# Scan parameters behind u's low parts and squares behind the casts, with TensorE's middle order held by a list

## The chip, the cores and the metric

The kernel runs on one core of a Trainium2 chip. The metric is the device time of one execution in microseconds (us), as the median of several runs; lower is better. The short names of the engines are those of the profile: PE is TensorE's matrix multiplication and PEld its weight load, DVE is VectorE, ACT is ScalarE, POOL is GpSimd, and SP issues most of the DMAs.

## The reference: what is computed

One hybrid decoder block on x with 256 rows of 1024 numbers, all in float32. Two branches run side by side on the same normed projection, are gated and added, and an MLP follows. Cut to what matters here:

```python
h = rms_norm(x, norm_mix_g);  proj = h @ w_in
q, k, v, u, g = split(proj)                       # u: 512 wide
o_a = attention(rotary(q), rotary(k), v)          # 8 heads of 128, causal
step = exp(log_step);  mag = exp(lam_re * step)   # the "scan parameters"
ar, ai = mag * cos(lam_im * step), mag * sin(lam_im * step)
s[t] = a * s[t-1] + c * (b @ u[t])                # 32 groups of 64 complex states
o_b = glu(gelu(real(c_out @ s) + d_skip * u))
x = x + (sigmoid(g_a) * o_a + sigmoid(g_b) * o_b) @ w_out
x = x + square(relu(rms_norm(x) @ w_up)) @ w_down
return rms_norm(x)
```

## The kernel before, in words

Every large product is made of three TensorE products. A weight block is loaded as float32 (tile `raw`), ScalarE rounds it to a high part (`hi`, line 83) and VectorE takes the rest as a low part (`lo`, line 84); the same is done to x (`xgh` on line 172, `xgl` on line 173). TensorE then adds hi by xgh, hi by xgl and lo by xgh. So each weight block costs a DMA, a ScalarE cast, a VectorE subtraction and then its matmuls, and four `hi`, four `lo` and five `raw` buffers turn over.

**Start (lines 117 to 194).** x, g and the weights of u come in first, in eight blocks k = 0 to 7 of 128 rows. The first block's weights come in two halves of 256 columns, the others in 512. `par` holds the scan's parameters (30 KB) and is issued on SP behind block 1's weights. For each block: xgh, xgl, the split of the weights, and 12 matmuls of 256 columns on u_acc (line 186) in the order hi by xgh, hi by xgl, lo by xgh. The squares of x for the norm (`sq`, lines 190 to 194) are ScalarE work, added up on VectorE; line 211 sums them on TensorE (`ms`), and lines 197 to 219 make the inverse root, mostly on POOL. Lines 221 and 222 (`rs_ps`) spread it over the partitions, line 225 copies it to `rs`, and line 239 multiplies u_acc with it to get u. Eight DMAs on ScalarE's queue (line 246) put u into the layout U2.

**Middle (lines 617 to 651).** The order of emission is the list ORDER: V is a half of v's projection (four weight blocks v0 to v3, then v4 to v7, 12 matmuls of 512 columns each), P and C are `prepare()`, the scan's parameters and matrices, T a table of sines, K the projections of q and k for two heads, S, A and G attention and gate, Q the scan of a quarter of the states, B the second gate. `prepare()` starts with some 70 VectorE operations on 128 by 16 numbers (helpers `ts` on lines 388 and 390, `tt` on line 395, `stt` on line 400), each of which mostly needs the one before it; then come multiplications of 128 by 256 (lines 456 to 461), copies to Bs (line 469), transposes `bt` on TensorE (line 486) and their copies W2 (line 487), which the scan's matmuls `x` (line 554) need together with U2.

**End.** glu, the output projection, the MLP's up and down projections, all three-part products as above.

The order on each engine is not written by hand: a scheduler puts the instructions in order with a model of their times and with priorities (a split has `high_priority(SPLIT_PRIO)`, so it goes ahead of other ready work), and the engines then run their lists strictly in that order. `behind(ins, others)` adds an order alone (no semaphore) and `after(...)` an order with a wait.

Of the kernel before, what the change touches and what calls it, by code (L numbers as in the profile page):

```python
# [8 lines left out]
F32 = mybir.dt.float32  # L9
# [34 lines left out]
QK = 2  # L44
ORDER = ("V0 V1 P0 T0 C0 Q0 T1 Q1 T2 K0 T3 X0 S0 G0 A0 G1 K1 K2 S1 Q2 A1 K3 G2 S2 A2 Q3 "
         "B0 G3 S3 X1 Y0 A3 B1")


def build(ctx, tc, dr, out):
    nc = tc.nc  # L50
    V, S, G, PE = nc.vector, nc.scalar, nc.gpsimd, nc.tensor

    keep = ctx.enter_context(tc.tile_pool(name="keep", bufs=1))
    ps = ctx.enter_context(tc.tile_pool(name="ps", bufs=1, space=PSUM))
# [26 lines left out]

    def split(hi, lo, x):
        ins = S.copy(hi, x).ins  # L83
        V.tensor_sub(lo, x, hi.bitcast(F32))  # L84
        return ins

    def mm3(o, wh, wl, xh, xl, first, last, **kw):
        PE.matmul(o, wh, xh, start=first, stop=False, **kw)  # L88
# [74 lines left out]
    V.memset(quarter, 0.25)  # L163
    sq = p1.tile([P, KD, T], F32, tag="yhl", name="sq")
    u_acc = ps.tile([P, 2, 2, T], F32, tag="x", name="u_acc")
    for c in range(4):
        wh = keep.tile([P, 1024], F32R, tag="hi", bufs=HI, name=f"hi_u{c}")
        wl = keep.tile([P, 1024], F32R, tag="lo", bufs=LO, name=f"lo_u{c}")
        for k2 in range(2):
            k, cols = 2 * c + k2, slice(k2 * 512, (k2 + 1) * 512)  # L170
            xk = xT[:, k, :] if k else x0
            S.activation(xgh[:, k, :], xk, AF.Copy, scale=g_mix[:, k : k + 1])
            V.scalar_tensor_tensor(xgl[:, k, :], xk, g_mix[:, k : k + 1],
                                   xgh[:, k, :].bitcast(F32), op0=ALU.mult, op1=ALU.subtract)
            if k:
                last = split(wh[:, cols], wl[:, cols], u_raw[c][:, cols])
                if k == 1:
                    second = last
            else:
                for i in range(2):  # L180
                    part = slice(i * 256, (i + 1) * 256)
                    split(wh[:, part], wl[:, part], u_raw[c][:, part])
            ws = [slice(k2 * 512 + m * P, k2 * 512 + (m + 1) * P) for m in range(4)]
            for i, (w, x) in enumerate(((wh, xgh), (wh, xgl), (wl, xgh))):
                for m in range(4):
                    PE.matmul(u_acc[:, m // 2, m % 2, :], w[:, ws[m]], x[:, k, :],  # L186
                              start=(k == 0 and i == 0 and m % 2 == 0),
                              stop=(k == KD - 1 and i == 2), skip_group_check=True)

    for i, xk in enumerate((x0, xT[:, 1, :])):  # L190
        S.activation(sq[:, i, :], xk, AF.Square)
    for c in range(1, 4):
        S.activation(sq[:, 2 * c : 2 * c + 2, :], xT[:, 2 * c : 2 * c + 2, :], AF.Square)
        V.tensor_add(sq[:, 0:2, :], sq[:, 0:2, :], sq[:, 2 * c : 2 * c + 2, :])


# [21 lines left out]
        rsqrt(G, rs_tok, rsm[:, 0:2], rsm[:, 4:6])  # L218
    V.tensor_scalar(rs_half, rs_tok, 0.5, None, op0=ALU.mult)
    rs_ps = att_bank("rs_ps")  # L220
    for h in range(2):
        PE.matmul(rs_ps[:, 0, h * P : (h + 1) * P], rs_tok[:, h : h + 1].to_broadcast([P, P]),
                  ident, start=True, stop=True)
# [27 lines left out]

    def proj_pair(first, name):
        acc = mm_bank(name)
        for j in range(2):
            wh, wl = in_unit(first + j, name)
            for k in range(KD):
                mm3(acc[:, j, :], wh[:, k * P : (k + 1) * P], wl[:, k * P : (k + 1) * P],
                    xgh[:, k, :], xgl[:, k, :], k == 0, k == KD - 1)
        return acc
# [18 lines left out]

    def tok_proj(first, name):
        other = first == 4  # L280
        acc = [flat(bank("y", 1, f"{name}{first}{h}") if other and h else
                    mm_bank(f"{name}{first}{h}")) for h in range(2)]
        for kk_ in range(4):
            wh, wl = in_unit(first + kk_, name)
            for k2 in range(2):
                k, w = 2 * kk_ + k2, slice(k2 * 512, (k2 + 1) * 512)
                for hf in range(2):
                    tok_mm(acc[hf], wh[:, w], wl[:, w], xgh, xgl, k, hf, k == 0, k == KD - 1)
        return acc
# [20 lines left out]

    def attn_head(q, k, j):
        s = att_bank("s").rearrange("p a b -> p (a b)")
        PE.matmul(s[:, 0:128], q[:, j, 0:128], k[:, j, 0:128], start=True, stop=False,
                  skip_group_check=True)
        PE.matmul(s[:, 0:128], ident_b, tri_b, start=False, stop=True, skip_group_check=True)
        PE.matmul(s[:, 128:384], q[:, j, 128:256], k[:, j, :], start=True, stop=False,
                  skip_group_check=True)
        PE.matmul(s[:, 256:384], ident_b, tri_b, start=False, stop=True, skip_group_check=True)
        st = p1.tile([P, 6], F32, tag="st", bufs=2, name="st")
        V.tensor_reduce(st[:, 0:1], s[:, 0:128], axis=mybir.AxisListType.X, op=ALU.max,  # L320
                        negate=True)
        V.tensor_reduce(st[:, 1:2], s[:, 128:384], axis=mybir.AxisListType.X, op=ALU.max,
                        negate=True)
        pr = p1.tile([P, 384], F32, tag="pr", bufs=2, name="pr")
        act(pr[:, 0:128], s[:, 0:128], AF.Exp, bias=st[:, 0:1],
                     accum_out=st[:, 2:3])
        act(pr[:, 128:384], s[:, 128:384], AF.Exp, bias=st[:, 1:2],
                     accum_out=st[:, 3:4])
        V.reciprocal(st[:, 4:6], st[:, 2:4])
        S.activation(pr[:, 0:128], pr[:, 0:128], AF.Copy, scale=st[:, 4:5])  # L330
        scaled.append(S.activation(pr[:, 128:384], pr[:, 128:384], AF.Copy, scale=st[:, 5:6]).ins)
        return pr

    def attn_pt(pr, last):
        pt = att_bank("pt").rearrange("p a b -> p (a b)")
        for i in range(3):
            after(PE.transpose(pt[:, i * P : (i + 1) * P], pr[:, i * P : (i + 1) * P], ident).ins,
                   last, "a head's transposes together")
        pts = p1.tile([P, 384], F32, tag="pts", bufs=2, name="pts")
        copied.append(S.copy(pts, pt[:, 0:384]).ins)  # L340
        return pts
# [3 lines left out]
    def attn_out(hp, prs, tha):  # L345
        pts = [attn_pt(x, [scaled[2 * hp + j]][: hp < 0]) for j, x in enumerate(prs)]
        o = att_bank("o")
        for j in range(2):
            hd = 2 * hp + j
            after(PE.matmul(o[:, j, :], v[:, 0, hd * P : (hd + 1) * P], pts[j][:, 0:256],  # L350
                             start=True, stop=False, skip_group_check=True).ins,
                   copied[-1:][: hp < 0], "a pair's outputs together")
            PE.matmul(o[:, j, 128:256], v[:, 1, hd * P : (hd + 1) * P], pts[j][:, 256:384],
                      start=False, stop=True, skip_group_check=True)
        V.scalar_tensor_tensor(mixA[:, 2 * hp : 2 * hp + 2, :], tha, 1.0, o,
                               op0=ALU.add, op1=ALU.mult)
# [13 lines left out]
    def prepare():  # L370
# [14 lines left out]
        def ts(x, s1, op0, s2=None, op1=None, o=None):  # L385
            o = t16() if o is None else o
            if op1 is None:
                V.tensor_scalar(o, x, s1, None, op0=op0)
            else:
                V.tensor_scalar(o, x, s1, s2, op0=op0, op1=op1)  # L390
            return o

        def tt(a, b, op):
            o = t16()
            V.tensor_tensor(o, a, b, op=op)
            return o

        def stt(a, s, b, op0, op1):
# [77 lines left out]
        for c in range(2):  # L476
            G.memset(Bs[c], 0.0)
            G.tensor_scalar(Bs[c][:, :, 0:32], bpad[:, c], 1.0, None, op0=ALU.mult)
            place(Bs[c], 32, ab[c], urgent=True)
        W2 = [keep.tile([P, 8, P], F32, tag=f"b4{c}", name=f"W2{c}") for c in range(2)]  # L480
        for c in range(2):
            bsp = Bs[c].rearrange("p (a b) k -> p a (b k)", b=2)
# [22 lines left out]
        Dt = p1.tile([P, 8, P], F32, tag="craw", name="Dt")  # L505
        G.memset(Dt, 0.0)
        dps = att_bank("dps").rearrange("p a b -> p (a b)").rearrange("p (m b) -> p m b", m=4)
        for m in range(4):
            for c, w_ in enumerate((Wr, nWi)):
                PE.matmul(dps[:, m, :], bpad[:, c, 4 * m : 4 * m + 4, :].rearrange("p a b -> p (a b)"),  # L510
# [34 lines left out]
    def ssm_quad(m):  # L545
        W2, mag2 = ssm[0], ssm[-3]
        cs, sn = tabs.pop(m)
        x = ps.tile([P, 2, 2, 2, P], F32, tag="x", name="x")
        xr, xi = [x[:, :, i].rearrange("p j h t -> p h j t") for i in range(2)]
        for h in range(2):  # L550
            for i in range(2):
# [26 lines left out]
        done = V.tensor_add(si, si, w).ins  # L578
        Wr, nWi, Dt = ssm[1:4]
        y = bank("y", 1, "y")  # L580
        for h in range(2):
            p = 2 * m + h
            after(PE.matmul(y[:, h, 0:P], Dt[:, p, :], U2[:, p, 1 : P + 1], start=(h == 0),
# [67 lines left out]
            tok_gate(32 + 4 * n, [thb[2 * n + i] for i in range(2)])  # L651


    mxh = keep.tile([P, KD, T], F32R, tag="b40", name="mxh")
    mxl = keep.tile([P, KD, T], F32R, tag="b41", name="mxl")

# [248 lines left out]
```

## Time and profile before

| | us |
|---|---|
| median of 3 runs (392.59 to 394.09) | 392.66 |
| the profiled execution's own time | 394.03 |
| its span, first to last instruction | 392.2 |
| PE busy | 382.8 (98%) |
| DVE busy | 288.7 (74%) |
| ACT busy | 231.8 (59%) |
| POOL busy | 29.6 (8%) |

The profiled execution has 1.8 us around its span and lies 1.37 us above the median, beside the slowest of the three runs. An instruction's row gives its start in us from the span's start and its length; in square brackets stands how long the engine had been idle before it and what ended that. A busy PE is modelled: the ends of its matmuls overlap the next ones, so the pace is read from one start to the next.

### The profile page before, as it was taken

The page shows a single profiled execution, that of the slowest core. Times are in us where ns is not written, and L with a number is a line of the kernel's source. Part 1 is how long each engine was busy: PE and PEld are TensorE (multiplying, and loading weights), DVE is VectorE, ACT ScalarE, POOL GpSimd, SP SyncE. Part 2 cuts the span into 40 slices and gives each one's busy share as a digit, 9 for nine tenths or more (in the row PEclk, how much of TensorE's full clock was granted, in tenths as well). Part 3 has the DMA queues.
Part 4 walks back from the last instruction along what each step waited for, and adds up shares of the span by engine and source line. Part 5 has one row for each costly group of instructions (what it writes and reads, how often), then busy time and mean ns, then how long its engine had stood idle before and what let it go on. Part 6 is the DMA issues. An engine that isn't in the chain of part 4 may idle for free.

```text
span 392.2 us, 6719 instructions
## 1 busy us (share of the span) xinstructions
PE 382.8 (98%) x2563; PEld 343.7 (88%) x2563; DVE 288.7 (74%) x501; ACT 231.8 (59%) x380; POOL 29.6 (8%) x35
## 2 busy tenths in 40 slices
PE   6999999999999999999999999999999999999993
PEld 3988999999999897888888999999999888888883
DVE  3999979999999997568839676767667444564434
ACT  6769899574554666954646665565555433444313
POOL 4242491000000000000000000000000000000000
PEclk9899999999999999999999999999999999999999
DMA  7993963445435155446486485655655555565202
GB/s 255 355 345 114 263 221 108 162 161 170 165 113 172 62 158 172 161 152 224 161 301 189 140 264 188 203 185 194 210 178 202 188 191 198 185 205 190 82 2 107
DMA packets 23199, 71.57 MB, mean 182 GB/s; under 512 B 2944, under 2 KB 5248, under 8 KB 23168
## 3 DMA queue, kind: packets, MB, share of 16 engines
q1 hardware_dynamic: 20144, 68.92, 51.5%
q10 hardware_dynamic: 3024, 2.23, 1.9%
q8 instruction: 20, 0.33, 0.3%
q14 instruction: 11, 0.09, 0.1%
HBM read 69.18 MB, written 1.05 MB: 179 GB/s over the span
## 4 chain that ended last, share of the span: by engine, by line
PE 92%; DMA 3%; DVE 3%; issue 1%; ACT 0%; SPq 0%; DVEq 0%
PE up L89 7%; PE up L88 7%; PE up L90 7%; PE dn L757 6%; PE dn L756 6%; PE dn L755 6%; PE u_acc L186 3%; DMA x2t<-x 2%; PE gb L272 2%; PE g L88 2%; PE k L88 2%; PE q L88 2%; PE g L89 2%; PE q L89 2%; PE v L272 2%; PE g L90 2%
## 5 line engine op out<-in xcount | busy, mean ns | idle before, releaser
L89 PE MATMUL up<-x2l,hi_up 128*128 128x256 f32 x256 | 70.7, 277 | 0.2 <-DVE x2l L718 0.2
L90 PE MATMUL up<-x2h,lo_up 128*128 128x256 f32 x256 | 70.5, 276 | 0.0
L88 PE MATMUL up<-x2h,hi_up 128*128 128x256 f32 x256 | 70.0, 276 | 0.0
L84 DVE TENSOR_TENSOR lo_dn<-raw_dn,hi_dn 128x1024 fp32r<-128x1024 f32 x32 | 39.2, 1225 | 40.4 <-ACT hi_dn L83 40.4
L83 ACT CAST hi_dn<-raw_dn 128x1024 fp32r<-128x1024 f32 x32 | 33.6, 1050 | 49.1 <-PE dn L757 24.6
L84 DVE TENSOR_TENSOR lo_up<-raw_up,hi_up 128x1024 fp32r<-128x1024 f32 x32 | 38.8, 1224 | 23.4 <-ACT hi_up L83 23.4
L83 ACT CAST hi_up<-raw_up 128x1024 fp32r<-128x1024 f32 x32 | 33.3, 1050 | 34.9 <-PE up L89 16.3
L89 PEld LDWEIGHTS up<-x2l,hi_up 128*128 128x128 f32 x256 | 48.1, 188 | 0.4 <-DVE x2l L718 0.4
L90 PEld LDWEIGHTS up<-x2h,lo_up 128*128 128x128 f32 x256 | 48.1, 188 | 0.0
L88 PEld LDWEIGHTS up<-x2h,hi_up 128*128 128x128 f32 x256 | 47.8, 188 | 0.1
L756 PE MATMUL dn<-lo_dn,hh 128*128 128x512 f32 x96 | 37.4, 389 | 0.0
L757 PE MATMUL dn<-hi_dn,hl 128*128 128x512 f32 x96 | 37.4, 389 | 0.0
L755 PE MATMUL dn<-hi_dn,hh 128*128 128x512 f32 x96 | 37.4, 389 | 0.0
L755 PEld LDWEIGHTS dn<-hi_dn,hh 128*128 128x128 f32 x96 | 18.0, 188 | 3.7
L756 PEld LDWEIGHTS dn<-lo_dn,hh 128*128 128x128 f32 x96 | 18.0, 188 | 3.7
L757 PEld LDWEIGHTS dn<-hi_dn,hl 128*128 128x128 f32 x96 | 18.0, 188 | 3.6
L88 PE MATMUL k<-xgh,hi_k 128*128 128x256 f32 x64 | 18.1, 283 | 0.0
L89 PE MATMUL k<-xgl,hi_k 128*128 128x256 f32 x64 | 18.1, 283 | 0.0
L88 PE MATMUL g<-xgh,hi_g 128*128 128x256 f32 x64 | 18.0, 281 | 0.0
L88 PE MATMUL q<-xgh,hi_q 128*128 128x256 f32 x64 | 17.9, 280 | 0.0
L90 PE MATMUL g<-xgh,lo_g 128*128 128x256 f32 x64 | 17.9, 280 | 0.0
L90 PE MATMUL k<-xgh,lo_k 128*128 128x256 f32 x64 | 17.9, 279 | 0.0
(274 smaller groups left out, 1018.9 us busy)
## 6 DMA issues: line engine op xcount, KB each, us to landing
raw_up<-w_up SPq DMA_DIRECT2D x32, 512.0 KB, 4.3
raw_dn<-w_down SPq DMA_DIRECT2D x32, 512.0 KB, 4.3
raw_v<-w_in SPq DMA_DIRECT2D x8, 512.0 KB, 5.5
raw_q<-w_in SPq DMA_DIRECT2D x8, 512.0 KB, 3.5
raw_k<-w_in SPq DMA_DIRECT2D x8, 512.0 KB, 3.3
raw_g<-w_in SPq DMA_DIRECT2D x8, 512.0 KB, 4.8
raw_gb<-w_in SPq DMA_DIRECT2D x8, 512.0 KB, 3.2
raw_glu<-w_glu SPq DMA_DIRECT2D x8, 512.0 KB, 3.5
```

The costliest lines, as they stand in the source:

```text
L83: ins = S.copy(hi, x).ins
L84: V.tensor_sub(lo, x, hi.bitcast(F32))
L88: PE.matmul(o, wh, xh, start=first, stop=False, **kw)
L89: PE.matmul(o, wh, xl, start=False, stop=False, **kw)
L90: PE.matmul(o, wl, xh, start=False, stop=last, **kw)
L186: PE.matmul(u_acc[:, m // 2, m % 2, :], w[:, ws[m]], x[:, k, :], start=(k == 0 and i == 0 and m % 2 == 0), stop=(k == KD - 1 and i == 2), ...
L272: PE.matmul(acc, xh[:, k, rows], wh, start=first, stop=False)
L755: PE.matmul(acc, xh, wh[:, w], start=(k == lead), stop=False, skip_group_check=True)
L756: PE.matmul(acc, xh, wl[:, w], start=False, stop=False, skip_group_check=True)
L757: PE.matmul(acc, xl, wh[:, w], start=False, stop=(k == end), skip_group_check=True)
```

## The change

Three things. (1) All `ts` and `tt` operations of `prepare()` are put in order behind the VectorE subtraction that makes the low part of u's second block (`second`, k = 1). `stt` and the others follow since they need results of these. (2) The squares of x on ScalarE are put behind casts of u's weights: those of blocks 0 and 1 behind block 0's last cast, those of a pair of later blocks behind the cast of the pair's second block. (3) TensorE's matmuls and transposes from v's first one to the end of the second gate's first part are recorded by name as they are emitted and chained, each behind the one before, in an order that a list of 934 instructions in runs gives. All the orders added are between instructions of one engine, with no semaphore.

```diff
+PE_ORDER = ("v*42 rs*2 v*44 bt*8 q*2 v*10 q*46 bt*8 x*2 k*48 g*13 dps*8 x*6 g*62 x*3 s*8 x*5 "
...
+class Listed:
+    def __init__(self, eng):
+        self.eng, self.name, self.of = eng, None, {}
+    def take(self, ins):
+        self.of.setdefault(self.name, []).append(ins.ins)
+        return ins
+    def matmul(self, *args, **kw):
+        return self.take(self.eng.matmul(*args, **kw))
...
-    V, S, G, PE = nc.vector, nc.scalar, nc.gpsimd, nc.tensor
+    V, S, G, PE = nc.vector, nc.scalar, nc.gpsimd, Listed(nc.tensor)
...
         ins = S.copy(hi, x).ins
-        V.tensor_sub(lo, x, hi.bitcast(F32))
-        return ins
+        return ins, V.tensor_sub(lo, x, hi.bitcast(F32)).ins
...
-                    split(wh[:, part], wl[:, part], u_raw[c][:, part])
+                    last = split(wh[:, part], wl[:, part], u_raw[c][:, part])
+            casts.append(last[0])
...
     for i, xk in enumerate((x0, xT[:, 1, :])):
-        S.activation(sq[:, i, :], xk, AF.Square)
+        behind(S.activation(sq[:, i, :], xk, AF.Square).ins, casts[:1], "weights first")
     for c in range(1, 4):
-        S.activation(sq[:, 2 * c : 2 * c + 2, :], xT[:, 2 * c : 2 * c + 2, :], AF.Square)
+        behind(S.activation(sq[:, 2 * c : 2 * c + 2, :], xT[:, 2 * c : 2 * c + 2, :],
+                            AF.Square).ins, [casts[2 * c + 1]], "weights first")
...
             if op1 is None:
-                V.tensor_scalar(o, x, s1, None, op0=op0)
+                ins = V.tensor_scalar(o, x, s1, None, op0=op0).ins
             else:
-                V.tensor_scalar(o, x, s1, s2, op0=op0, op1=op1)
+                ins = V.tensor_scalar(o, x, s1, s2, op0=op0, op1=op1).ins
+            behind(ins, second[1:], "the first weights' parts first")
...
-            V.tensor_tensor(o, a, b, op=op)
+            behind(V.tensor_tensor(o, a, b, op=op).ins, second[1:],
+                   "the first weights' parts first")
...
+    before = []
+    for run in PE_ORDER.split():
+        name, n = run.split("*")
+        for _ in range(int(n)):
+            ins = PE.of[name].pop(0)
+            behind(ins, before, "TensorE's order")
+            before = [ins]
```

## Rows read from the trace of the kernel before

**Rows 1.** Waits of PE, whole span: who for whom, total us, times, longest.

```profile
PE u_acc L186 <- DVE lo_u L84: 1.5, 2, 0.9
PE u_acc L186 <- ACT hi_u L83: 0.4, 2, 0.2
PE up L89 <- DVE x2l L718: 0.2, 1, 0.2
```

**Rows 2.** Busy time by stretch; columns as in the first line.

```profile
core 0: us, PE busy (x) PEld busy (x) DVE busy (x) ACT busy (x) POOL busy (x), PEclk, DMA share, GB/s
5.60:8.90 3.30, 1.82 (x10) 1.41 (x11) 2.14 (x13) 2.19 (x5) 0.00 (x0) 1.00 0.97 323
9.00:12.30 3.30, 3.30 (x18) 3.30 (x17) 3.30 (x10) 3.30 (x8) 0.00 (x0) 0.50 1.04 381
12.40:20.00 7.60, 7.60 (x69) 7.60 (x68) 7.60 (x17) 5.38 (x9) 2.66 (x2) 1.00 0.89 341
20.00:52.00 32.00, 32.00 (x184) 27.52 (x184) 30.86 (x103) 27.90 (x59) 14.41 (x18) 1.00 0.73 247
```

**Rows 3.** Timeline of DVE, 3.5 to 9 us: start, us, instruction, idle before.

```profile
3.98 0.48 DVE L173 SCALAR_TENSOR_TENSOR xgl<-xg,xgh 128x256 fp32r<-128x256 f32 x1 [2.78 <-ACT xgh L172]
6.76 0.17 DVE L390 TENSOR_SCALAR s<-par 128x16 f32<-128x16 f32 x1 [2.29 <-DMA par<-par]
...
7.02 0.42 DVE L84 TENSOR_TENSOR lo_u<-raw_u,hi_u 128x256 fp32r<-128x256 f32 x1
7.35 0.17 DVE L390 TENSOR_SCALAR s<-s 128x16 f32<-128x16 f32 x1
...
7.51 0.48 DVE L173 SCALAR_TENSOR_TENSOR xgl<-xT,xg,xgh 128x256 fp32r<-128x256 f32 x1
7.91 0.17 DVE L388 TENSOR_SCALAR s<-s 128x16 f32<-128x16 f32 x1
...
8.15 0.36 DVE L84 TENSOR_TENSOR lo_u<-raw_u,hi_u 128x256 fp32r<-128x256 f32 x1
8.43 0.17 DVE L400 SCALAR_TENSOR_TENSOR s<-s,s 128x16 f32<-128x16 f32 x1
...
8.58 0.69 DVE L84 TENSOR_TENSOR lo_u<-raw_u,hi_u 128x512 fp32r<-128x512 f32 x1
```

**Rows 4.** Timeline of ACT, 3.8 to 7.2 us.

```profile
3.85 0.40 ACT L191 ACTIVATE sq<-xg 128x256 f32<-128x256 f32 x1
4.16 0.39 ACT L83 CAST hi_u<-raw_u 128x256 fp32r<-128x256 f32 x1
...
5.17 0.39 ACT L83 CAST hi_u<-raw_u 128x256 fp32r<-128x256 f32 x1
6.55 0.62 ACT L83 CAST hi_u<-raw_u 128x512 fp32r<-128x512 f32 x1 [0.99 <-DMA raw_u<-w_u]
```

**Rows 5.** Timeline of PE, 7 to 9 us.

```profile
7.49 0.51 PE L186 MATMUL u_acc<-xgh,lo_u 128*128 128x256 f32 x2 [0.90 <-DVE lo_u L84]
8.57 0.50 PE L186 MATMUL u_acc<-xgh,lo_u 128*128 128x256 f32 x2 [0.57 <-DVE lo_u L84]
```

**Rows 6.** Chain that ended last: start, us, what.

```profile
30.73 0.45 PE rs_ps L222 x4
```

**Rows 7.** Timeline of DVE, 28 to 39 us.

```profile
28.15 0.17 DVE L219 TENSOR_SCALAR rs_half<-rsm 128x2 f32<-128x2 f32 x1 [0.66 <-POOL rsm L206]
...
37.04 1.22 DVE L84 TENSOR_TENSOR lo_v<-raw_v,hi_v 128x1024 fp32r<-128x1024 f32 x1
38.17 1.28 DVE L239 TENSOR_TENSOR u<-u_acc,xg 128x512 f32<-128x512 f32 x2
```

**Rows 8.** Timeline of PE, the first matmul on that low part of v.

```profile
38.34 0.47 PE L273 MATMUL v<-lo_v,xgh 128*128 128x512 f32 x1
```

**Rows 9.** Line 246, the DMAs that lay u out: ns, first and last start; landing.

```profile
L246 ACTq DMA_DIRECT2D U<-u x8: 593/616/751, 39.5 to 44.4; - x8
...
DMA to landing us min/median/max: 2.1/5.5/6.2
```

**Rows 10.** Timeline of PE, 50 to 51.5 us.

```profile
50.80 0.49 PE L554 MATMUL x<-U,W 64*128 64x128 f32 x4
```

More of the change, by code (lines that the diff above doesn't have):

```diff
@@ L46, with transpose @@
          "B0 G3 S3 X1 Y0 A3 B1")
+PE_ORDER = ("v*42 rs*2 v*44 bt*8 q*2 v*10 q*46 bt*8 x*2 k*48 g*13 dps*8 x*6 g*62 x*3 s*8 x*5 "
[4 rows of a table added]
+class Listed:
[6 more added lines that the diff above has]
+        return self.take(self.eng.matmul(*args, **kw))
+    def transpose(self, *args, **kw):
+        return self.take(self.eng.transpose(*args, **kw))
 def build(ctx, tc, dr, out):
     nc = tc.nc
-    V, S, G, PE = nc.vector, nc.scalar, nc.gpsimd, nc.tensor
+    V, S, G, PE = nc.vector, nc.scalar, nc.gpsimd, Listed(nc.tensor)
     keep = ctx.enter_context(tc.tile_pool(name="keep", bufs=1))
@@ L165, in build @@
     u_acc = ps.tile([P, 2, 2, T], F32, tag="x", name="u_acc")
+    casts = []
     for c in range(4):
@@ L220, in build @@
     rs_ps = att_bank("rs_ps")
+    PE.name = "rs"
     for h in range(2):
@@ L253, in proj_pair @@
         acc = mm_bank(name)
+        PE.name = name
         for j in range(2):
@@ L280, in tok_proj @@
         other = first == 4
+        PE.name = name
         acc = [flat(bank("y", 1, f"{name}{first}{h}") if other and h else
@@ L312, in attn_head @@
         s = att_bank("s").rearrange("p a b -> p (a b)")
+        PE.name = "s"
         PE.matmul(s[:, 0:128], q[:, j, 0:128], k[:, j, 0:128], start=True, stop=False,
@@ L335, in attn_pt @@
         pt = att_bank("pt").rearrange("p a b -> p (a b)")
+        PE.name = "pt"
         for i in range(3):
@@ L347, in attn_out @@
         o = att_bank("o")
+        PE.name = "o"
         for j in range(2):
@@ L479, in prepare @@
             place(Bs[c], 32, ab[c], urgent=True)
+        PE.name = "bt"
         W2 = [keep.tile([P, 8, P], F32, tag=f"b4{c}", name=f"W2{c}") for c in range(2)]
@@ L507, in prepare @@
         dps = att_bank("dps").rearrange("p a b -> p (a b)").rearrange("p (m b) -> p m b", m=4)
+        PE.name = "dps"
         for m in range(4):
@@ L548, in ssm_quad @@
         x = ps.tile([P, 2, 2, 2, P], F32, tag="x", name="x")
+        PE.name = "x"
         xr, xi = [x[:, :, i].rearrange("p j h t -> p h j t") for i in range(2)]
@@ L580, in ssm_quad @@
         y = bank("y", 1, "y")
+        PE.name = "y"
         for h in range(2):
@@ L651, in build @@
             tok_gate(32 + 4 * n, [thb[2 * n + i] for i in range(2)])
+    before = []
[5 more added lines that the diff above has]
+            before = [ins]
+    PE.name = "later"
     mxh = keep.tile([P, KD, T], F32R, tag="b40", name="mxh")
```

4 rows, old and new, of the table PE_ORDER are left out of this document.

## The prediction

> **What bounds the kernel now.** I read PE's waits first. In the whole span they are three: 1.5 us for low parts of u's weights, 0.4 us for high parts, 0.2 us at the MLP's start [rows 1]. The first two lie before 9 us; from then on PE has no idle time to win but the 0.2 us. So the kernel is TensorE's list of matmuls, run without a gap from 8.57 us on, and this change can only win what lies ahead of that: gaps before 8.57 us [rows 5], and the stretch of 9.0 to 12.3 us in which the granted clock is half [rows 2].
>
> Next comes the question why the low parts are late. VectorE's timeline answers it [rows 3]: after xgl of block 0 at 3.98 us it stands idle for 2.29 us, released by the landing of `par`, since its list has three parameter operations ahead of the first low part. The casts that the low parts need were there long before (4.16 and 5.17 us, [rows 4]). So a 30 KB transfer holds the first weights.
>
> Then I read who else is full. VectorE is busy for all of 9.0 to 20.0 us and for 30.86 of 32 us after that [rows 2]; its one gap there is 0.66 us for POOL at 28.15 us [rows 7]. Two engines have no air in the same 40 us, so a gain on PE alone doesn't count: it must be asked what PE meets next that VectorE makes.
>
> **The change part by part.**
>
> Squares. On ACT the two first squares take a slot of about 0.31 us each (3.85 to 4.16 us, [rows 4]) ahead of the casts. Without them block 0's first cast starts at 3.85 and its second at 5.17 - 0.61 = 4.56 us. Block 1's cast waits for its DMA until 6.55 us and stays there [rows 4]; the two squares fit in the 0.99 us of idle time before it, so they cost nothing. If the scheduler puts them elsewhere, they cost 0.6 us of ACT, which has 5.38 of 7.60 us busy in 12.4 to 20.0 [rows 2]. Later squares only change places with casts.
>
> Parameters. Behind the new order VectorE makes block 0's two low parts and block 1's xgl as soon as the casts end (by about 5.6 us: 0.35 + 0.40 + 0.35 us of slots from 4.5 us on), then waits for block 1's cast, which ends at 6.55 + 0.62 = 7.17 us. Block 1's low part starts at 7.2 instead of 8.58 us: 1.38 us earlier. But the nine parameter operations that stood ahead of it are not gone; they run behind it. Their slots, from start to start [rows 3], are 6.76 to 7.02, 7.35 to 7.51, 7.91 to 8.15 and 8.43 to 8.58: 0.26 + 0.16 + 0.24 + 0.15 = 0.81 us. So VectorE's queue is ahead by 1.38 - 0.81 = 0.57 us from then on, and not by the 2.29 us of its wait. Queued behind the held operations is nothing but their own chain; who waits for that is `prepare()`.
>
> TensorE, start. Block 0's low products no longer wait (they stand at 7.49 and 8.57 us, [rows 5]); block 0 is done by about 6.4 us, PE then waits some 0.8 us for block 1's cast, and by 9.0 us it has done 26 of u's 96 matmuls where it had done 13. At the pace of the full clock (69 matmuls in 7.60 us, [rows 2], 0.110 us each) 13 matmuls are 1.43 us. That is PE's own lead if the clock falls to half in the same stretch as now.
>
> The clock. It was granted at half in 9.0 to 12.3 us, behind a stretch in which PE was busy for 1.82 of 3.30 us, and came back behind one in which it had no gap [rows 2]. At half, 18 matmuls ran in 3.30 us; at full it would be 30: 12 x 0.110 = 1.3 us to win if it doesn't fall. Closing the gaps makes PE busy for some 2.3 of those 3.30 us (10 more matmuls, less those cut off): nearer to full, not full. The Trainium skill, "TensorE: Matmul & The Clock Gate", section "HAM oscillation — how this bites in real kernels", says that idle gaps between bursts of matmuls put the clock back to half and that keeping the engine fed avoids it; by that the 1.3 us would come on top. The trace agrees so far as the one fall here follows the one stretch with gaps; no row shows how much busy time is enough. The sum takes the fall as it is.
>
> The list. Counted along PE's timeline from v's first matmul, the order of before is the list's, run for run: 42 of v, then rs_ps (four rows for two instructions of the list, [rows 6]), 44 of v, 8 of bt, and so on. So it costs nothing and moves nothing by itself. It does take a freedom away: VectorE's and ACT's lists are made anew around an order of PE that can't give way.
>
> **Where the gain ends.** PE's lead of 1.43 us lasts until v's seventh weight block. Its low part is made at 37.04 to 38.26 us [rows 7], and PE takes it at 38.34 us [rows 8]: 0.08 us of slack. VectorE is ahead by 0.57 us there, for everything between is its own back-to-back work, and the POOL wait at 28.15 us moves along, as POOL starts from VectorE's own operations. So PE can be early by at most 0.57 + 0.08 = 0.65 us, and the other 0.78 us comes back as a new wait of PE. The next such place allows little more: the last of the eight DMAs that lay u out starts at 44.4 us [rows 9] and with 5.5 to 6.2 us to land arrives at 49.9 to 50.6 us; PE takes it at 50.80 [rows 10], 0.2 to 0.9 us later, and it hangs on VectorE's multiplication at 38.17 us [rows 7]. That is a limit of 0.77 to 1.47 us. Behind that everything starts from PE's or VectorE's own work and shifts along.
>
> Sum: 394.03 - 0.65 = 393.4 us for the profiled execution; it lies 1.37 us over the median of the runs, so on the median 392.66 - 0.65 = **392.0 us**.
>
> What no row shows is where the scheduler now puts the nine operations and the work behind them. From below: if the table work and multiplications that stood ahead of v's seventh low part fall behind it, PE keeps its whole 1.43 us. From above: if u's two multiplications (1.28 us, [rows 7]) come ahead of that low part, it is late by 1.28 - 0.65 = 0.6 us. I take the place as it is, since the splits have priority now as before.
>
> **The rivals.**
>
> Weights first all the way: VectorE's splits keep up, and PE keeps 1.43 us: 391.2 us. For it: the parameter chain starts later, so more of it lies behind the splits. Against it: u's DMAs, which hang on rs and on VectorE as before.
>
> The clock stays up: 1.43 + 1.3 = 2.7 us on PE's side, 389.9 us at best; it too needs VectorE's places to open, wider than in the second case, so I take 390.5, between the two.
>
> Slower, the list against a later chain: the parameters start at 7.9 instead of 6.76 us, their long chain and with it the tables on ACT come later, and some operation ahead of v's seventh low part, or of u's layout, takes the room. It decides once more than 0.65 us of other work is put ahead of that low part: PE, whose order can't give way, waits for the excess. With u's multiplications the price is 0.6 us (393.3 us); with one more table operation of about 0.7 us 394.0; if other places in the saturated stretch follow, 395.
>
> That the change doesn't do what it says: `stt` has no order of its own, but each such operation needs a result of one that has. I give it nothing.
>
> **How the numbers follow.** The forecast (0.3 to 1.1 us won) 0.47; weights first 0.21; the clock 0.10; slower 0.22. A measurement of this kernel tells about 0.5% (1.96 us) from no change, which is below 390.70 or above 394.62. Only the clock's case and a part of the second reach below: 0.15. Of the slower case about half gets over 394.6: 0.12. The rest, 0.73, is the same. The range of 8 in 10 takes in the clock's likelier time and the slower case with one table operation: 390.4 to 394.1.
>
> **What would show it.** Right: block 1's low part on VectorE near 7.2 us; PE's waits for u's low parts gone and one of about 0.8 us for block 1's high part in their place; u's last matmul near 18.5 us; a new wait of PE for a low part of v near 37.7 us, some 0.8 us long, and no other up to the MLP. Wrong: no such wait (then VectorE's order changed and 391 is near); waits of PE for q's or k's low parts, for U2 or in the attention (then 394); a granted clock of 1.00 from 9 us on; or a time that moves with `par`'s landing, which differs between runs and which I have from one.

## The result and the profile after

| | before | after |
|---|---|---|
| median (range), us | 392.66 (392.59 to 394.09) | 402.56 (402.25 to 403.66) |
| ratio, 95% interval | 1 | 1.0242 [1.0205, 1.0279] |
| the profiled execution's own time | 394.03 | 402.25 |
| its span | 392.2 | 400.2 |
| PE's waits behind the first 4 us | 2.1 | 9.9 |

The change makes the kernel 9.9 us slower. The two profiled executions differ by 8.2 us; the one of before stands 1.37 us over its median, that of after 0.31 us under. In the kernel after, a helper records every TensorE instruction, so all matmuls have line L65 and all transposes L68; the split is L105 (high) and L106 (low).

Waits of PE, whole span of the kernel after (who for whom, total us, times, longest), to hold against [rows 1]:

```profile
PE bt L68 <- issue: 6.5, 1, 6.5
PE gb L65 <- DVE tha L390: 3.4, 1, 3.4
PE hot L65 <- DVE quarter L184: 1.2, 1, 1.2
```

The waits for u's parts are gone, as intended (the `hot` wait is the warm-up before 4 us, and stands in both kernels). Two new ones have come, and both lie where the prediction saw none. Busy time by stretch of the kernel after, against [rows 2]:

```profile
core 0: us, PE busy (x) PEld busy (x) DVE busy (x) ACT busy (x) POOL busy (x), PEclk, DMA share, GB/s
5.60:8.90 3.30, 3.30 (x24) 3.18 (x24) 2.32 (x9) 2.41 (x6) 0.00 (x0) 1.00 1.03 359
9.00:12.30 3.30, 3.30 (x31) 3.30 (x30) 3.30 (x11) 3.30 (x8) 0.00 (x0) 1.00 1.04 406
40.80:47.50 6.70, 2.74 (x12) 2.67 (x13) 6.63 (x14) 6.66 (x16) 0.40 (x1) 0.50 0.69 202
```

The front did better than forecast: no gap in 5.6 to 8.9 us, and the granted clock stays at 1.00 in 9.0 to 12.3 us. The half clock is now in 40.8 to 47.5 us. VectorE's timeline of the kernel after at the start, against [rows 3]:

```profile
3.98 0.48 DVE L195 SCALAR_TENSOR_TENSOR xgl<-xg,xgh 128x256 fp32r<-128x256 f32 x1 [2.79 <-ACT xgh L194]
4.39 0.42 DVE L106 TENSOR_TENSOR lo_u<-raw_u,hi_u 128x256 fp32r<-128x256 f32 x1
5.12 0.42 DVE L106 TENSOR_TENSOR lo_u<-raw_u,hi_u 128x256 fp32r<-128x256 f32 x1
6.12 0.69 DVE L106 TENSOR_TENSOR lo_u<-raw_u,hi_u 128x512 fp32r<-128x512 f32 x1 [0.58 <-ACT hi_u L105]
6.73 0.17 DVE L420 TENSOR_SCALAR s<-par 128x16 f32<-128x16 f32 x1
```

The low parts stand ahead of the first parameter operation, and that one starts at 6.73 us, no later than before (6.76, [rows 3]). So the parameters are not late at the start. They are late at the end of their chain. First VectorE, ScalarE and PE of the kernel before around it, then the same operations of the kernel after:

```profile
35.93 0.42 DVE L458 TENSOR_TENSOR ab<-ab,cw 128x256 f32<-128x256 f32 x1
37.36 0.81 ACT L469 COPY Bs<-ab 64x256 f32<-64x256 f32 x2
41.18 1.03 PE L486 MATMUL bt<-cst,Bs 128*128 128x128 f32 x8
```

```profile
29.32 1.21 DVE L106 TENSOR_TENSOR lo_v<-raw_v,hi_v 128x1024 fp32r<-128x1024 f32 x1
...
33.54 1.28 DVE L264 TENSOR_TENSOR u<-u_acc,xg 128x512 f32<-128x512 f32 x2
34.74 0.41 DVE L265 SCALAR_TENSOR_TENSOR rcos<-cst,xg 128x256 f32<-128x256 f32 x1
35.07 0.41 DVE L266 SCALAR_TENSOR_TENSOR rsin<-cst,xg 128x256 f32<-128x256 f32 x1
...
36.09 1.22 DVE L106 TENSOR_TENSOR lo_v<-raw_v,hi_v 128x1024 fp32r<-128x1024 f32 x1
...
40.62 1.22 DVE L106 TENSOR_TENSOR lo_q<-raw_q,hi_q 128x1024 fp32r<-128x1024 f32 x1
41.76 0.41 DVE L490 TENSOR_TENSOR ab<-ab,cw 128x256 f32<-128x256 f32 x1
43.86 0.80 ACT L501 COPY Bs<-ab 64x256 f32<-64x256 f32 x2
44.76 1.94 PE L68 MATMUL bt<-cst,Bs 128*128 128x128 f32 x8 [6.46 <-issue]
```

The first subtraction on `ab` is 5.83 us late, the copy to Bs 6.50 us. Before, u's multiplications, rcos and rsin stood behind that subtraction (38.17 us and on, [rows 7]), as did the last two low parts of v (37.04 and 40.37 us) and every one of q. Now six of these stand ahead of it: v's seventh and eighth low part (29.32 and 36.09 us), u's multiplications, rcos, rsin and one low part of q, with slots of 1.13, 1.14, 1.20, 0.33, 0.34 and 1.14 us: 5.28 us. The 0.55 us that are left of the 5.83 aren't broken down here; 0.67 more come on ScalarE, which had other work when `ab` was there. "Issue" names nothing as the releaser; the copy to Bs, which `bt` reads, ends at 43.86 + 0.80 = 44.66 us and PE goes on at 44.76, so that copy is taken as what it waited for. Before, the copy ended at 38.17 us, 3.0 us ahead of `bt`.

The second wait, in the second gate. Rows of PE and VectorE, first of the kernel before, then of the one after:

```profile
126.45 0.39 PE L272 MATMUL gb<-hi_gb,xgh 128*128 128x512 f32 x1
...
128.84 0.69 DVE L360 TENSOR_TENSOR tha<-g,xg 128x512 f32<-128x512 f32 x1
```

```profile
130.90 0.40 PE L65 MATMUL gb<-hi_gb,xgl 128*128 128x512 f32 x1
134.72 0.47 PE L65 MATMUL gb<-hi_gb,xgh 128*128 128x512 f32 x1 [3.43 <-DVE tha L390]
...
133.89 0.69 DVE L390 TENSOR_TENSOR tha<-g,xg 128x512 f32<-128x512 f32 x1
```

`gb` is made in two halves of the tokens, each in a PSUM bank of its own. Both kernels multiply `tha` out of a bank of g some 3 us after `gb` has begun (125.65 to 128.84 us before, 130.33 to 133.89 after). Before, the 4th matmul of `gb` followed at once, since PE first ran 19 matmuls on one half; now the 4th belongs to the other half and waits for that multiplication to free a bank.

**Where the time went**, along PE in the two profiled executions. The work ahead of `bt` (86 of v's 96 matmuls, and rs_ps) ends at 38.30 us (44.76 - 6.46) instead of 41.18: 2.88 us won. The wait for Bs costs 6.46, so `bt` is 3.58 us late. The granted clock is at half until 47.59 us, so 2.83 us of matmuls behind the wait run at half pace: 1.4 us more. The wait in `gb`: 3.43. The sum is -2.88 + 6.46 + 1.4 + 3.43 = 8.4 us; the spans differ by 8.0.

### The profile page after: what moved, and what is told of

Same layout as the page of the kernel before. It is cut to its first block, busy times and chain, and to the rows that moved or that the text cites. A ratio compares the mean times of both kernels' runs of the same rounds, so it can differ in the third digit from the quotient of the medians.

```text
span 400.2 us, 6713 instructions
## 1 busy us (share of the span) xinstructions
PE 382.9 (96%) x2563; PEld 343.8 (86%) x2563; DVE 291.3 (73%) x501; ACT 233.6 (58%) x380; POOL 24.8 (6%) x35
## 4 chain that ended last, share of the span: by engine, by line
PE 88%; DVE 6%; issue 3%; DMA 1%; ACT 1%; ACTq 0%; DVEq 0%
PE up L65 22%; PE dn L65 16%; PE v L65 6%; PE glu L65 5%; PE wo L65 5%; PE gb L65 5%; PE g L65 4%; PE q L65 4%; PE dnw L65 4%; PE k L65 3%; PE u_acc L65 3%; PE dnq L65 1%; PE y L65 1%; PE s L65 1%; PE o L65 1%
## 5 line engine op out<-in xcount | busy, mean ns | idle before, releaser
L65 PE MATMUL up<-x2l,hi_up 128*128 128x256 f32 x256 | 70.6, 277 | 0.0
L65 PE MATMUL up<-x2h,lo_up 128*128 128x256 f32 x256 | 70.5, 276 | 0.0
L65 PE MATMUL up<-x2h,hi_up 128*128 128x256 f32 x256 | 70.1, 276 | 0.0
L106 DVE TENSOR_TENSOR lo_dn<-raw_dn,hi_dn 128x1024 fp32r<-128x1024 f32 x32 | 39.2, 1225 | 40.4 <-ACT hi_dn L105 40.4
L105 ACT CAST hi_dn<-raw_dn 128x1024 fp32r<-128x1024 f32 x32 | 33.6, 1049 | 49.1 <-PE dn L65 24.6
L106 DVE TENSOR_TENSOR lo_up<-raw_up,hi_up 128x1024 fp32r<-128x1024 f32 x32 | 38.9, 1225 | 24.2 <-ACT hi_up L105 24.2
L105 ACT CAST hi_up<-raw_up 128x1024 fp32r<-128x1024 f32 x32 | 33.3, 1049 | 35.0 <-PE up L65 16.3
L65 PEld LDWEIGHTS up<-x2l,hi_up 128*128 128x128 f32 x256 | 48.1, 188 | 0.0
L65 PEld LDWEIGHTS up<-x2h,lo_up 128*128 128x128 f32 x256 | 48.1, 188 | 0.0
L65 PEld LDWEIGHTS up<-x2h,hi_up 128*128 128x128 f32 x256 | 47.8, 188 | 0.1
L65 PE MATMUL dn<-lo_dn,hh 128*128 128x512 f32 x96 | 37.4, 389 | 0.0
L65 PE MATMUL dn<-hi_dn,hl 128*128 128x512 f32 x96 | 37.4, 389 | 0.0
L65 PE MATMUL dn<-hi_dn,hh 128*128 128x512 f32 x96 | 37.4, 389 | 0.0
L65 PEld LDWEIGHTS dn<-hi_dn,hh 128*128 128x128 f32 x96 | 18.0, 188 | 3.8
L65 PEld LDWEIGHTS dn<-lo_dn,hh 128*128 128x128 f32 x96 | 18.0, 188 | 3.7
L65 PEld LDWEIGHTS dn<-hi_dn,hl 128*128 128x128 f32 x96 | 18.0, 188 | 3.6
L65 PE MATMUL glu<-hi_glu,yhl 128*128 128x512 f32 x64 | 20.6, 397 | 0.0
L65 PE MATMUL q<-xgh,hi_q 128*128 128x256 f32 x64 | 18.1, 283 | 0.0
L65 PE MATMUL k<-xgh,hi_k 128*128 128x256 f32 x64 | 18.1, 282 | 0.0
L65 PE MATMUL k<-xgl,hi_k 128*128 128x256 f32 x64 | 18.0, 282 | 0.0
L65 PE MATMUL q<-xgl,hi_q 128*128 128x256 f32 x64 | 18.0, 281 | 0.0
L65 PE MATMUL g<-xgh,hi_g 128*128 128x256 f32 x64 | 17.9, 280 | 0.0
```

The lines of the kernel that those rows point to most:

```text
L65: return self.take(self.eng.matmul(*args, **kw))
L106: return ins, V.tensor_sub(lo, x, hi.bitcast(F32)).ins
```

## The experiments

The first theory is that the list itself costs, through `gb`. The second is that the change makes VectorE's list anew, and that the order there is what costs. All twelve compute the whole result; each ratio is to runs of the kernel before on the same chip beside it. Diffs are to the kernel after, unless they say otherwise.

**e1: everything but the list.**

```diff
-    for run in PE_ORDER.split():
-        ...
-            behind(ins, before, "TensorE's order")
```

> Both new orders on VectorE and ScalarE stay, TensorE's list of 934 instructions is taken out, so the scheduler orders TensorE itself. Theory A (the held list makes PE wait for bt while the first Bs comes late, 6.5 us at 38 us and 3.6 us at 131 us): both waits are gone and the lead at v's start (3 to 4 us) is kept in part, 388 to 392 us. Rival B (the late chain of scan parameters costs by itself, whatever PE's order): PE waits elsewhere for the same work and the time stays at 398 us or more.

397.31 us, 1.0102 [1.0055, 1.0149]. Without the list the edits at the front still cost a per cent: PE waits 2.9 us at `gb` (for the multiplication of q) and 1.4 us for a low part of q. So the list is a part of the loss, not all of it. The time lies between the two readings of the expectation. The wait at `bt` is gone, since PE now takes q first (41.22 us, `bt` at 47.14).

**e2: the list alone, with neither front edit.**

```diff
-        behind(S.activation(sq[:, i, :], xk, AF.Square).ins, casts[:1], "weights first")
+        S.activation(sq[:, i, :], xk, AF.Square)
...
-            behind(ins, second[1:], "the first weights' parts first")
+            pass
...
-            behind(V.tensor_tensor(o, a, b, op=op).ins, second[1:],
-                   "the first weights' parts first")
+            V.tensor_tensor(o, a, b, op=op)
```

> The list alone, with neither of the two new orders. Theory A (list and late chain only cost together): as before, 392 to 394 us, no PE wait of over 1 us behind 10 us. Rival C (the list costs by itself, for within one name it takes the order of emission and not that of the kernel before): over 396 us.

399.01 us, 1.0137 [1.0095, 1.0178]. PE of this run around `gb`, and the stretch behind the wait (columns as above):

```profile
125.96 0.40 PE L65 MATMUL gb<-hi_gb,xgl 128*128 128x512 f32 x1
129.25 0.47 PE L65 MATMUL gb<-hi_gb,xgh 128*128 128x512 f32 x1 [2.89 <-DVE tha L389]
```

```profile
129.90:133.20 3.30, 3.30 (x10) 2.54 (x9) 3.30 (x7) 2.05 (x5) 0.00 (x0) 0.50 0.34 137
```

The list is not free: it has the `gb` wait of the kernel after, with a clock at half behind it, by itself: up to that wait, VectorE's and ScalarE's instructions come in the order of the kernel before.

**e3 and e4: the list with one front edit each** (the parameters; the squares).

> List and the order of the scan parameters, squares as before. VectorE's list has ab behind seven low parts of v and u's multiplications, where before it had six and none. If the held parameters are what makes bt late: PE waits 3 to 6 us before bt and the time is 397 to 402 us. If it is the squares: 391 to 394 us.

> List and the order of the squares, parameters as before. VectorE's list has ab behind all eight low parts of v, u's multiplications and one low part of q, as in the changed kernel. If the squares, through the scheduler's new list for VectorE, make bt late: PE waits 5 to 7 us before bt, 400 to 403 us. If only the held parameters do: 391 to 394 us.

e3: 399.12 us, 1.0146 [1.0084, 1.0209]; PE waits 0.3 us at `bt`, 1.7 at `gb`, and 1.2, 1.1 and 0.7 in other places. e4: 403.31 us, 1.0248 [1.019, 1.0306]; 4.0 us at `bt`, 2.4 at `gb`. The late Bs comes with the squares, which the prediction had put at nothing; with the parameters alone, the time is that of the list alone (1.0137). For e3 the expectation had tied such a time to a long wait at `bt`, which didn't come; the runs of both are spread, and their intervals overlap.

**e5 and e6: the list made exact.** Each matmul of v and gb is recorded under its half, and the list names the halves in the order of before; e5 has both front edits, e6 the parameters alone.

```diff
-PE_ORDER = ("v*42 rs*2 v*44 bt*8 ... x*8 gb*19 s*4 y*10 gb*18 pt*1 ..."
+PE_ORDER = ("v00*3 v01*3 v00*3 ... x*8 gb320*19 s*4 y*10 gb321*18 pt*1 gb320*1 ..."
...
                 for hf in range(2):
+                    PE.name = f"{name}{first}{hf}"
```

> The changed kernel with a list that names the two halves of v and of gb apart, so that TensorE's middle order is that of the kernel before instruction for instruction; both new orders stay. Theory A (the order within gb makes PE wait 3.6 us at 131 us and drops the clock behind it; the late ab makes it wait 6.5 us before bt): the wait at gb is gone, the one before bt stays at 5 to 7 us, 397 to 400 us beside a kernel before of 393.5. Rival B (gb waits because the stall before bt has shifted VectorE against PE): gb's wait stays, 402 us.

> The same list by halves, with the order of the parameters alone; the squares stand as before. With the list as written this kernel waited 0.3 us before bt and 1.7 us at gb. Theory A: both small or gone, 1.2 us of wait at the first transposes of the attention may stay: 392 to 395 us, within 0.5% of the kernel before. If the parameters' order costs by itself: 396 us or more.

e5: 399.99 us, 1.0157 [1.013, 1.0184]. e6: 396.62 us, 1.0077 [1.0052, 1.0103]. PE's waits, first of e5 and then of e6:

```profile
PE bt L72 <- issue: 5.8, 1, 5.8
```

```profile
PE bt L72 <- issue: 1.2, 1, 1.2
PE pt L72 <- ACT pr L362: 1.2, 1, 1.2
PE s L69 <- DVE k L335: 0.7, 1, 0.7
```

The `gb` wait is gone in both, so what was wrong there was the order of the halves. From 1.0242 to 1.0157 that is 0.0085, or 3.3 us, about as long as the wait was (3.43). PE still waits 5.8 us at `bt` with the squares and 1.2 without. e6 stays slower than the kernel before by 0.0077, which is 3.0 us, and its three waits are 3.1: the second reading of its expectation. No run has this exact list with neither edit, so what the list by halves costs by itself is open.

**e7: e5 with `bt` put later in the list** (behind q's 46 matmuls and into k's 48).

```diff
-  bt*8 q*2 v40*2 ... q*46 bt*8 x*2 k*48 g*13 dps*8 x*6
+  q*2 v40*2 ... q*46 bt*8 k*24 bt*8 k*24 g*13 dps*8 x*8
```

> The list by halves, both new orders, and in the list the two runs of bt moved back: the first behind q's 46 matmuls, the second into the middle of k's 48, and the first two matmuls on x to the other six. VectorE's order is left to the scheduler. Theory A (PE waits before bt only because the list puts it ahead of q and k, whose low parts are there): no wait of over 1.5 us before 60 us, the lead of some 3.5 us at 38 us is kept up to there; 388 to 392 us beside a kernel before of 393.5. If what is late there holds up other work as well (x, the scan, y), the lead is lost behind 60 us: 394 to 398 us.

399.13 us, 1.0143 [1.011, 1.0176]. PE begins q 3.77 us sooner (38.20 us for 41.97), of which 0.79 is `bt`, which now comes later (41.18 to 41.97 before); so it is 3.0 us ahead. It loses that at a low part of q (0.74 us) and at the second run of `bt`, behind which the clock is at half:

```profile
54.98 1.94 PE L72 MATMUL bt<-cst,Bs 128*128 128x128 f32 x8 [4.04 <-ACT W L525]
...
145.71 0.38 PE L69 MATMUL g<-xgh,lo_g 128*128 128x256 f32 x1 [1.90 <-DVE lo_g L110]
```

Neither reading of the expectation (388 to 392, 394 to 398 us) is met. So it isn't the place of `bt` in the list alone: the scan's whole preparation is late on VectorE and ScalarE, and the next step that needs it waits.

**e8 and e9: the front with every other order held.** Here the instructions of VectorE, ScalarE and TensorE are recorded and chained, from the first to the last, in the order that each engine had in the kernel before, except for the front: e8 has both edits, e9 only the nine parameter operations of [rows 3] put behind block 1's low part. To the kernel before:

```diff
-    V, S, G, PE = nc.vector, nc.scalar, nc.gpsimd, nc.tensor
+    V, S, G, PE = Rec(nc.vector), Rec(nc.scalar), nc.gpsimd, Rec(nc.tensor)
...
+    for eng, text in ((V, D_ORDER), (S, A_ORDER), (PE, T_ORDER)):
+        ...
+                behind(eng.made[i], last, "an engine's order")
```

> The kernel before with the orders of TensorE, VectorE and ScalarE held instruction for instruction over the whole program, but for the change's two edits at the start: VectorE's nine parameter operations behind the low part of u's block 1, and ScalarE's squares behind the casts. Theory A (the two edits win what the start's sums give, and all that was lost came through the orders made anew): low part of block 1 near 7.2 us, PE 1.4 us or more ahead at v's start, a new wait of some 0.8 us before v's seventh low part, 0.6 us won in all, 392.9 beside a kernel before of 393.5; no other new wait. Rival B (the edits themselves push the chain of parameters so far back that PE waits before bt whatever the order): a wait of 2 us or more before bt, 395 us or more.

> The same, with ScalarE's order as before, so that only the nine parameter operations are moved. Theory A: VectorE's gain is set by block 1's cast at 7.17 us, which the squares don't move, so the result is that of the kernel with both edits, 392.9, within 0.3 us. If the squares' 0.6 us on ScalarE count: 0.3 to 0.6 us more than with both.

e9: 392.52 us, 0.9974 [0.9948, 1.0000], which is 1.0 us under the kernel before (393.48 beside it); the interval just reaches no change. Rows of e9, VectorE, then PE, then the stretch of 9 to 12.3 us (columns as above):

```profile
6.17 0.69 DVE L110 TENSOR_TENSOR lo_u<-raw_u,hi_u 128x512 fp32r<-128x512 f32 x1 [0.27 <-ACT hi_u L110]
6.78 0.17 DVE L110 TENSOR_SCALAR s<-par 128x16 f32<-128x16 f32 x1
...
8.63 0.68 DVE L110 TENSOR_TENSOR sq<-sq 128x512 f32<-128x512 f32 x1
...
35.58 1.22 DVE L110 TENSOR_TENSOR lo_v<-raw_v,hi_v 128x1024 fp32r<-128x1024 f32 x1
...
36.84 0.50 PE L110 MATMUL v<-lo_v,xgh 128*128 128x512 f32 x1 [0.88 <-DVE lo_v L110]
```

```profile
9.00:12.30 3.30, 3.30 (x28) 3.13 (x28) 3.30 (x9) 3.30 (x8) 0.00 (x0) 1.00 1.05 411
```

This is the prediction's case: the waits for low parts of u are gone, and PE gives its lead back at v's seventh low part in a new wait of 0.88 us. That matmul starts 1.50 us sooner than in [rows 8], and the lead lasts: the span is 390.5 us for 392.2, where the profiled execution of before lies 1.37 us over its median.

e8: 394.08 us, 1.0026 [1.0007, 1.0045]. Its VectorE:

```profile
10.05 0.69 DVE L110 TENSOR_TENSOR sq<-sq 128x512 f32<-128x512 f32 x1 [1.16 <-ACT sq L110]
10.66 0.68 DVE L110 TENSOR_TENSOR lo_u<-raw_u,hi_u 128x512 fp32r<-128x512 f32 x1
```

With the squares behind the casts, VectorE's sum of two squares (line 194 of the kernel before, at 8.63 us in e9) waits for them until 10.05, and block 2's low part stands behind it: PE then waits 1.3 us for a low part of u. It waits 1.4 us more at v's seventh low part, and 1.1 at the MLP's start, where VectorE stood waiting for a DMA of x. No wait at `bt` comes, so the expectation's rival B falls, but the forecast 392.9 isn't met, and against both readings for e9 the squares make the pair slower than e9. Even so e8 stands 0.0131 under e5, which has the same two front edits and, through the middle, the same PE order. What differs is whether the other lists, VectorE's and ScalarE's above all, may be made anew. TensorE's order behind the listed middle is free in e5 too, but that costs nothing: from the last matmul of `gb` to the last of all e5 takes 224.0 us, the kernel before 224.1. This is the second theory's test, and it holds; which of the two engines' lists it is, no run tells apart.

**e10 and e11: the list of VectorE rearranged by hand.** 32 operations between v's sixth and k's first low part are put in another order, with v's and q's low parts sooner; e10 has both front edits, e11 the parameters alone.

> Both edits and all orders held, and 32 of VectorE's operations between v's sixth and k's first low part in another order: low parts 6 and 7 of v, both of q, and u's multiplications go ahead of table and matrix work that nobody waits for yet. Theory A (VectorE's place of v's seventh low part is what caps the lead): that wait goes, PE keeps 1.0 to 1.5 us up to x near 50 us; 391.9 to 392.5 beside a kernel before of 393.5. If another wait takes its place behind 50 us (s, gb or lo_g): the gain falls back to 0.5 us or less.

> The whole computation. The orders of VectorE, ScalarE and TensorE are the kernel before's, but for two things on VectorE: the nine parameter operations stand behind block 1's low part (as in the run that moved them alone: 0.9974 of the time before), and the 32 operations between v's sixth and k's first low part are put in the order of the run that moved them with the squares (1.0029). If what that run lost came with the squares, this one keeps the lead through v: the wait of 0.9 us at v's seventh low part goes, and the time is 0.9974 or up to 0.9 us below that (0.995 to 0.9975). If the new order of the 32 itself makes VectorE late further on (that run waited 1.2 us at gb for the multiplication of q, and 0.5 us at bt for Wr), the same waits stand here with the lead before them, and the time is 0.998 to 1.002.

e10: 394.09 us, 1.0029 [1.0011, 1.0047]. e11: 393.23 us, 0.9989 [0.9960, 1.0018]. e10 waits 1.1 us for a low part of u, 1.2 at `gb` and 0.5 at `bt`; the 391.9 to 392.5 us of its first reading aren't met. PE's waits of e11:

```profile
PE u_acc L110 <- ACT hi_u L110: 1.5, 3, 0.8
PE gb L110 <- DVE q L110: 1.2, 1, 1.2
```

The wait at v's seventh low part is gone, and PE is 1.67 us ahead at 48 us; 1.1 us of that are lost again at `gb`, 75 us on, where VectorE's multiplication of q is the late one. The second reading of e11's expectation is the right one: in this trace, moving the room to the splits only moves the wait. By the times alone e11 can't be told from e9.

**e12: the squares alone, all else held.**

> The whole computation. The orders of all three engines are the kernel before's, but for ScalarE's first squares, which stand behind the casts; the parameter operations stay where they were. Theory that the squares are what spoils the front: VectorE's sum of two squares now comes due before its inputs, and the low parts of u behind it are late; TensorE waits some 1 to 1.3 us for a low part of u near 10 us, none of it is won back, and the time is 1.002 to 1.005. Rival, as forecast (squares have slack, the casts come earlier): no wait over 0.3 us at u's low parts beside those of before, and the time is 0.998 to 1.001.

394.08 us, 1.0007 [0.9983, 1.0032]. PE waits 0.9 us in two places for low parts of u (the longest 0.6), and 1.1 us at the MLP's start as in e8; the time can't be told from the kernel before. So holding every order costs nothing that can be seen either, though no run holds them with neither edit. The theory that the squares spoil the front by themselves falls: they do so only where VectorE is early, as in e8.

## Why the prediction was wrong

392.0 us (390.4 to 394.1) was forecast, 402.56 measured. Step by step:

**The bound and the front: right.** The two front edits take away PE's waits for u's parts. With the other orders held (e9) the forecast wait at v's seventh low part came, 0.88 us for the 0.78 forecast, and the gain of 0.65 us was 1.0 by the medians (0 to 2 by the interval). Block 1's low part stood at 6.12 us (after) and 6.17 (e9) and not at 7.2, since its weights were there sooner: its cast ran at 5.49 us in the profiled execution of after, at 6.55 in that of before [rows 4]. With that, the prediction's own sum for e9 is 8.58 - 6.17 - 0.81 = 1.60 us of lead for VectorE; 37.04 [rows 7] - 35.58 = 1.46 were measured. That the wait came out so near is luck: VectorE was ahead by 1.46 us and not 0.57, and PE by 2.54 us just before that matmul (35.34 us for 37.88) and not 1.43.

**The clock: the value taken was wrong, and the rival right.** I took the fall at 9 us as it was. It didn't come in the kernel after or in e9. In the kernel after PE was 2.9 us ahead where `bt` should begin, and lost it all there. Nor does the fall belong to the old front: in e2, which has that front, `par` let VectorE go at 5.63 us, PE waited 0.2 us for parts of u, and the granted clock was 1.00 in 9.0 to 12.3 us. Its last four matmuls of u begin at 18.21 us, for 19.59 in the profiled execution of before and 17.03 in e9, so 1.4 of those 2.6 us came with the execution and not with the edit. A time that moves with `par`'s landing was one of the prediction's own signs of being wrong.

**"So it costs nothing and moves nothing by itself": the first step that failed.** I compared the list with before run for run by name. But `gb` is a name for two accumulations in two banks, and a name's matmuls go in the order of emission, which alternates the halves. The scheduler had not kept that order. Alone the list takes the time to 1.0137 (e2), where the prediction had nothing; its `gb` wait is 3.43 us in the kernel after, and naming the halves takes it away (e5).

**"I take the place as it is": the second, and in the kernel after the larger.** The sum had been made on VectorE's old list, though the text itself said that the list is made anew. e5 against e8 prices that choice at 0.0131, some 5 us. The place that it watched, v's seventh low part, came sooner and not later: 29.32 us for 37.04 [rows 7], with no wait of PE for any part of v. So far the rival "weights first all the way" came true. What paid for it is the chain behind the splits, and the sum had no term for that.

**The slower rival: PE's wait was right, its place and price were not.** "PE, whose order can't give way, waits for the excess" is what happened. But I looked for it at one consumer, v's seventh low part, and priced it at 0.6 us with u's multiplications. Those came ahead of `ab` instead, and with them low parts of v and q. The chain that got late was Bs and `bt`, whose slack in the kernel before was 3.0 us; that slack isn't in the prediction at all. Lateness of 6.50 us less 3.0 is 3.5 us, as found (`bt` is 3.58 us late). PE met it with a lead of 2.88 us, so the wait was 6.46. And a wait of PE has a second price that I left out, the half clock behind it, 1.4 us here.

**"So they cost nothing" (the squares): wrong in the kernel, right by itself.** Held, they cost nothing that can be measured (e12), though with the parameters moved as well the kernel is slower with them than without (1.0026 for 0.9974, e8 and e9). Free, they come with the late Bs: e4 over e3 by 0.0102 (the intervals overlap), e5 over e6 by 0.0080 (they don't). Why the scheduler then puts `ab` behind more low parts isn't settled by these runs. That the casts, and with them the splits, come due sooner in its model is a guess; no run here shows its reckoning.

**The parameters' start** was not later (6.73 for 6.76 us); "the parameters start at 7.9 instead of 6.76 us" was wrong, and the slower rival didn't need it.

## What to carry to other kernels

Where a scheduler makes the lists, an edit's cost is not that of the instructions it names: hold every engine's order as it was, make the edit alone, and only then let the lists go free. An order written down by name must name what the hardware tells apart (each accumulation and its bank), or it isn't the order that it copies. Before an engine's order is fixed, list the slack of each of its consumers in the stretch, and price a late producer at the one with the least, with the clock that a stall costs.

## What the runs showed of the hardware

**A stall of PE may halve the clock behind it, but in these runs its length doesn't say whether.** In e2 a wait of 2.89 us was followed by a granted clock of 0.50 in 129.83 to 133.24 us, with matmuls of 512 columns 0.43 us apart instead of 0.23. In e7 such stretches came with the waits of 4.04 and 1.90 us (54.47 to 57.89, 146.63 to 150.05), and others with 2.89 us in e1, 4.04 and 2.40 in e4 and 5.78 in e5. In the kernel after, the wait of 6.46 us brought one of 40.76 to 47.59 us, but behind the wait of 3.43 us in `gb` the clock stayed up:

```profile
131.40:134.70 3.30, 0.00 (x0) 0.01 (x1) 3.30 (x7) 2.17 (x7) 0.00 (x0) 1.00 0.45 159
134.80:138.00 3.20, 3.20 (x14) 2.63 (x15) 3.20 (x6) 1.37 (x2) 0.00 (x0) 1.00 0.43 164
```

The Trainium skill, "TensorE: Matmul & The Clock Gate", section "HAM oscillation — how this bites in real kernels", tells of a kernel in which TensorE waits for a transfer between bursts and starts each next burst at the low clock. Of the nine waits of 1.9 us or more in the kernel after and e1 to e7, eight agree with it, the 3.43 us in `gb` does not. Behind 1.69 us (e3) and 1.43 us (e8) the clock stayed up as well. At the start much shorter waits had half clock behind them in two executions (0.90 and 0.57 us before [rows 5], 0.35 and 0.39 us in e4, at half from 7.44 to 10.86 us), and in e12 0.59 and 0.28 us had none.

**When block 1's weights and `par` arrive differs between executions by more than the gain at stake.** Block 1's cast started at 5.49, 5.68, 5.98, 6.41 and 6.55 us (after, e8, e11, e12, before), and `par` let VectorE go at 5.63 us in e2 and at 6.76 before [rows 3].
